# Attention on five engines: both heads of a pair in one store, and the whole order planned anew

## The chip, the cores and the metric

The kernel runs on one core of one Trainium2 chip. The metric is the device time of one execution in microseconds (us). The profile gives, for one profiled execution, every instruction's place in time on the core's engines: TensorE (PE; PEld is its weight load), VectorE (DVE), ScalarE (ACT), GpSimd (POOL), and the queue of SyncE (SP), which issues most of the DMA transfers.

## The reference

Softmax attention over 64 heads (8 x 8), each with 512 queries and keys of 64 elements:

```python
scores = np.einsum('bhqd,bhkd->bhqk', q, k) * scale
scores = scores - scores.max(axis=-1, keepdims=True)
attn = np.exp(scores)
attn = attn / attn.sum(axis=-1, keepdims=True)
return np.einsum('bhqk,bhkd->bhqd', attn, v).astype(np.float32)
```

## The kernel before

The 64 heads are worked in 32 pairs. Of each pair the kernel loads q, k and v (256 KB each, both heads, seven pairs deep), casts them to 16 bit on GpSimd, transposes q and k on TensorE (`transposes`) and copies them out of PSUM on VectorE (`copy`, tile `tqk`). A block of scores is 128 keys by 512 queries of one head. Two blocks make a *group*; there are 128 whole groups, of which the last is done in two halves. TensorE writes a group's scores to one of three PSUM buffers (`st`, line 575), and it is then exponentiated in one of two ways:

- On ScalarE, in one instruction (line 579), which writes `pt`. 112 groups go this way, three of them in the opening part (line 777).
- On VectorE, for the 16 groups listed in `Plan.ON_DVE`: `raise_` (line 599) reads the scores from PSUM and makes 16-bit integers; five passes (lines 616 to 639) make two factors, `pe` and `pd`, of them, in 16-bit data in SBUF. TensorE multiplies with both factors, so such a block costs it a second matmul.

TensorE then multiplies by v with a column of ones attached, so that each row also gets its sum (line 680). A head's result has four *units* (128 queries each); seven units share a PSUM bank, and two such banks are shared with the transposes. VectorE takes the reciprocals of the sums (line 645, `rc`) and multiplies by them (line 650), which writes into `ring`, a buffer in SBUF of `NU` = 112 units, 28 heads. From there `store` (line 658) sends heads out, in the order in which they were worked (`heads`). The last head has its own end (lines 709, 710 and 716). Heads are not always worked in the order of their numbers.

Nothing in this order is left to a scheduler. The class `Plan` steps through time with costs written into it, decides on each step what each engine does next, and returns one list of steps; the kernel then emits the steps in that order, and each engine's queue runs its instructions in just that order, waiting where data or a buffer is not there. Plan's constants hold these costs and some preferences: how late a reciprocal or a copy may be before it goes ahead of a pass (`LATE_NORM`, `LATE_COPY`), when scores are issued early (`HURRY`, `SOON`, `BACKLOG`), what a load and a store take (`LOAD`, `STORE`), and by when a cast of k and q or of v is due (`DUEK`, `DUEV`, `DUEL`). `step_sp` decides what SP issues: a load whose buffer has become free goes first, unless more than `URGENT` stores are waiting, and stores fill the places between. `room` keeps a product of line 650 from being planned before the store that frees its place in the ring. Casts on GpSimd are tied to an instruction of VectorE by `cast_behind`, since the two can hinder each other.

Of the kernel before, what the change touches and what calls it, by code (L numbers as in the profile page):

```python
# [17 lines left out]
class Plan:  # L18
# [15 lines left out]
    STEP = 5  # L34
    CALM, KEEN = 9000, 4
    FIRST_UNIT = 4
    ON_DVE = (5, 11, 15, 24, 36, 41, 49, 55, 60, 70, 76, 83, 94, 105, 109, 120)

    LATE_NORM, LATE_COPY, HURRY, SOON, BACKLOG = 2300, 700, 1000, 200, 700
    LATE_MUL, WAIT = 400, 200  # L40
    SLACK, AHEAD = 0, 2

    CAST, CAST_PORT, CAST_DONE, TO_POOL = 557, 475, 130, 150
    SCALE_PORT, PRODUCT_PORT, GAP, REACH = 271, 537, 20, 5
    FIRST_LAND, LOAD, STORE, LATENCY, ISSUE = 5200, 740, 370, 2300, 470
    QUEUED, URGENT = 3500, 16
    PAIRED = (3, 13)
    RAW, QK16, NV, NU = 7, 5, 12, 112
    PAIR, DUEK, DUEV, DUEL, PRE = 3300, 2800, 4000, 7000, 0

    def __init__(self, groups, pairs, first):
        self.groups, self.pairs = groups, pairs
        self.pe, self.act, self.dve = 7000, self.FIRST_EXP, 6300
        self.pool, self.port, self.dma = 4600, 4600, self.FIRST_LAND
        self.m, self.tiled = first, True
        self.read = []
        self.exps = {}
        for m in range(first):
            self.act += self.EXP + self.EXP_FIXED
            self.exps[m] = self.act + self.EXP_DONE  # L60
            self.read.append(self.exps[m])
        self.tq = {0: 5800}
        self.transposed = {0: 5800}
        self.next_t = 1
        self.part_t = 0
        self.banks = [5100, 5800]
        self.todo = [(g, h) for g in range(pairs) for h in range(2)]
        self.last = self.todo.pop()
        self.last_part = 0
        self.head = None  # L70
        self.units = self.FIRST_UNIT
        self.member = {b: m for m, grp in enumerate(groups) for b in grp}
        self.ready = []
        self.passes = []
        self.passed = {}
        self.raised = set()
        self.steps = []
        self.busy_dve = 0
        self.done_heads = 0

        late = {grp[0][0] for m, grp in enumerate(groups) if m in self.ON_DVE}
        due = []
        for g in range(pairs):
            scores = 5000 + self.PAIR * g
            if g:
                due += [(scores - self.DUEK, g, "k"), (scores - self.DUEK + 10, g, "q")]
            due.append((scores + self.DUEV + (self.DUEL if g in late else 0), g, "v"))
        self.due = sorted(due)
        self.uncast = list(self.due)
        self.casts = []  # L90
        self.landed, self.cast_done = {}, {}
        self.first_loads = [(g, n) for _, g, n in self.due if g < self.RAW]
        self.first_loads += [(self.RAW, "k"), (self.RAW, "q")]
        for x in self.first_loads:
            self.dma += self.LOAD
            self.landed[x] = self.dma
        self.loads, self.stores, self.stored = [], [], []
        self.sp = 1650 + 470 * len(self.first_loads)
# [55 lines left out]
    def step_sp(self, t):  # L154
        if self.sp > t or (self.loads and self.dma > t + self.QUEUED):
            return
        urgent = len(self.stores) > self.URGENT
        if self.loads and not urgent:
            g, n = self.loads[0]
            if self.cast_done.get((g - self.RAW, n), 1e9) <= t:  # L160
                self.loads.pop(0)
                self.note(t, "load", g, n)
                self.dma = max(self.dma, t + self.LATENCY - self.LOAD) + self.LOAD
                self.landed[(g, n)] = self.dma
                self.sp = t + self.ISSUE
                return
        if self.stores and self.stores[0] <= t:
            self.stores.pop(0)
            self.note(t, "store")
            self.dma = max(self.dma, t + self.LATENCY - self.STORE) + self.STORE  # L170
            self.stored.append(self.dma)
            self.sp = t + self.ISSUE

    def room(self, t, u):
        heads = (u - self.NU - self.FIRST_UNIT + 3) // 4
# [9 lines left out]
    def for_dve(self, m):  # L185
        return m in self.ON_DVE

# [69 lines left out]
    def head_values(self, t):  # L257
        if self.m <= self.KEEN:
            return False
        if self.head is None:  # L260
            for g, h in self.todo[:14]:
                if t >= self.wants(g, h, 0):
                    break
            else:
                return False
            if self.edge() and self.bank(t) is None:
                return False
            self.todo.remove((g, h))
            self.head = (g, h, 0)
        g, h, part = self.head  # L270
        if t < self.wants(g, h, part):
            return False
        if self.edge():
            n = self.bank(t)
            if n is None:
                return False
            self.banks[n] = 1e9
            self.bank_v = n
            self.begun = self.units
        self.note(t, "values", g, h, part, self.units, self.bank_v)  # L280
        more = sum(self.for_dve(self.member[(g, c, h)]) for c in range(4))
        self.full(t, self.V_UNIT + self.EXTRA * more)
        self.units += 1
        if self.edge():
            what = (self.begun, self.units - self.begun, self.bank_v)
            self.ready.append((self.pe + self.TO_DVE, "rec", what))
        self.head = (g, h, part + 1) if part < 3 else None
        return True
# [119 lines left out]
def kernel(  # L408
# [7 lines left out]
    nc = tc.nc  # L416
    B, H, S, D = q.shape
    P = 128
    NI = S // P
# [30 lines left out]
    NU = Plan.NU  # L450
    ring = cpool.tile([P, NU, D], FP32, name="ring")
# [10 lines left out]
    heads = []  # L462
# [4 lines left out]
    def source(src, g):  # L467
        b, h = g // ppb, 2 * (g % ppb)
        return src[b, h : h + 2].rearrange("h (p i) d -> p h i d", i=NI)
# [185 lines left out]
            )  # L655
        )

    def store():

        g, h, u0 = heads.pop(0)  # L660
        left = 2 * NP - 1 - (u0 + NI - Plan.FIRST_UNIT) // NI
        queue = nc.scalar if left < 2 else nc.sync
        u = u0 % NU
        if g in Plan.PAIRED and h == 0:
            return
        if g in Plan.PAIRED:
            both = ring[:, u - NI : u + NI, :].rearrange("p (h i) d -> p h i d", h=2)
            queue.dma_start(out=source(out, g), in_=both)
        else:
            queue.dma_start(out=source(out, g)[:, h], in_=ring[:, u : u + NI, :])  # L670

    def values(g, h, y, u, bank):

# [143 lines left out]
    with tc.manual_schedule():  # L817
        plan = Plan(groups, NP, 3)
        steps = plan.run()
        first_loads()  # L820
        for g, name in plan.first_loads:
            load(g, name)
        make_identity(nc, ident)
        for n in range(NV):
            nc.vector.memset(vps[n][:, :, :, D : D + 1], 1.0)
        first_pair()
        do = {
            "transposes": transposes,
            "scores": scores,
            "values": values,  # L830
            "load": load,
            "store": store,
            "cast": cast_behind,
            "raise": raise_,
            "copy": lambda g, b: copy(g),
            "pass": pass_,
            "last": last_values,
            "finish": finish,
            "rec": lambda u, n, b: reciprocal(u, n),
            "mul": lambda u, n, b: normalise(u, n),  # L840
        }
        for what, *args in steps:
            do[what](*args)
# [30 lines left out]
```

## Time and profile before

| | |
|---|---|
| three runs | 113.86, 114.5 and 114.7 us; median 114.5 |
| the profiled execution | 114.31 us, its span 112.5 us (first to last instruction) |
| granted TensorE clock | 0.999 of full speed |
| busy, PE / DVE / ACT / POOL | 104.0 / 101.3 / 105.6 / 65.2 us |
| moved | 33.84 MB, 301 GB/s over the span |

Instructions of an engine are drawn with some overlap (the next begins before the last has ended), so a group's mean duration is longer than what it holds the engine for. The latter is read from the distance between ends or from the chain of waits, which splits the time without overlap. In the slices, a 9 is a slice with 90% or more. In the timeline a row gives the start, the time to the end of the last of its instructions, the engine, the line, what it writes and reads, and how many there are; in brackets stands the idle time ahead of it and what ended that.

### The profile page before, as it was taken

To read this page: it belongs to the slowest core of one execution; us is meant where nothing else is said; L and a number is where in the kernel's file an instruction comes from. 1 tells how busy PE (TensorE), PEld (TensorE's weight loads), DVE (VectorE), ACT (ScalarE), POOL (GpSimd) and SP (SyncE) were. 2 spreads that over 40 slices of the span, in tenths; PEclk is the share of its full clock that TensorE was granted. 3 is DMA by queue.
4 is the path that set the end of the run, shared out by engine and by line. 5 is a ranking of instruction groups with operands and counts; after the bars stand their busy time and mean duration, and the time that the engine had idled before them with its cause. 6 is when DMAs were issued, how large, how long until landed. Compare 5 with 4: busy or idle time off the path is not lost.

```text
span 112.5 us, 4427 instructions
## 1 busy us (share of the span) xinstructions
PE 104.0 (92%) x1731; PEld 71.1 (63%) x1731; DVE 101.3 (90%) x226; ACT 105.6 (94%) x118; POOL 65.2 (58%) x127
## 2 busy tenths in 40 slices
PE   7988889899999998999999999999999999999970
PEld 7654546576775564657677557678667765776560
DVE  1547999999989999999999999999999999999760
ACT  4689999999999999999999999999999999999960
POOL 2166788265478866686847888755868796000000
PEclk9999999999999999999999999999999999999999
DMA  2999999999999999999999999999997976848435
GB/s 90 271 340 354 346 349 349 342 349 348 348 329 331 344 350 347 344 353 325 283 299 376 346 312 363 358 374 353 357 305 229 289 244 212 270 143 268 159 99 184
DMA packets 35349, 33.84 MB, mean 301 GB/s; under 512 B 2560, under 2 KB 35328, under 8 KB 35328
## 3 DMA queue, kind: packets, MB, share of 16 engines
q1 hardware_dynamic: 34752, 33.04, 90.8%
q10 hardware_dynamic: 576, 0.52, 1.4%
q8 instruction: 13, 0.21, 0.8%
q14 instruction: 8, 0.07, 0.2%
HBM read 25.17 MB, written 8.39 MB: 298 GB/s over the span
## 4 chain that ended last, share of the span: by engine, by line
DVE 45%; PE 42%; ACT 7%; issue 2%; DMA 1%
PE o L680 18%; PE st L575 14%; DVE pd L599 10%; DVE tqk L548 8%; DVE ring L650 8%; ACT pt L579 7%; PE tp L535 6%; DVE m L633 4%; DVE pd L639 3%; PE st_0a L727 3%; DVE pe L625 3%; DVE m L616 2%; DVE m L635 2%; DVE rc L645 2%; DMA out_dram<-ring 1%
## 5 line engine op out<-in xcount | busy, mean ns | idle before, releaser
L579 ACT ACTIVATE pt<-st 128x1024 f16<-128x1024 f32 (+1 forms) x110 | 100.3, 1114 | 0.0
L680 PEld LDWEIGHTS <-pt 128*128 128x128 f16 x880 | 38.9, 98 | 12.3 <-issue 10.6
L680 PE MATMUL o<-vp,pt 128*128 128x65 f16 x880 | 46.3, 194 | 0.2
L575 PE MATMUL st<-tqk 64*128 64x512 f16 (+1 forms) x250 | 42.4, 381 | 2.9 <-ACT pt L579 1.7
L504 POOL CAST qkp<-k 128x512 f16<-128x512 f32 x31 | 21.5, 692 | 12.2 <-DMA k<-in_k_dram 5.2
L494 POOL CAST vp<-v 128x512 f16<-128x512 f32 x32 | 21.8, 695 | 7.7 <-DVE rc L645 2.6
L504 POOL CAST qkp<-q 128x512 f16<-128x512 f32 x30 | 21.1, 703 | 6.6 <-DVE rc L645 2.2
L650 DVE TENSOR_TENSOR ring<-o,rc 128x448 f32<-128x448 f32 (+2 forms) x37 | 22.3, 606 | 0.6
L680 PE MATMUL o<-vp,pe 128*128 128x65 f16 x128 | 22.1, 195 | 0.0
L680 PE MATMUL o<-vp,pd 128*128 128x65 f16 x128 | 21.9, 193 | 0.0
L548 DVE COPY tqk<-tp 128x1024 f16<-128x1024 f16 x30 | 20.3, 677 | 0.2 <-PE tp L535 0.2
L535 PE MATMUL tp<-ident,qkp 128*128 128x128 f16 x248 | 19.5, 219 | 0.9 <-DVE ring L650 0.7
L599 DVE TENSOR_SCALAR pd<-st 128x1024 uint16<-128x1024 f32 x16 | 19.5, 1217 | 0.7 <-PE st L575 0.7
L575 PEld LDWEIGHTS <-tqk 64*128 64x128 f16 x250 | 11.7, 93 | 12.3 <-issue 4.8
L535 PEld LDWEIGHTS <-qkp 128*128 128x128 f16 x248 | 14.3, 97 | 7.3 <-issue 4.4
L680 PEld LDWEIGHTS <-pe 128*128 128x128 f16 x128 | 12.5, 97 | 3.8 <-issue 2.9
L680 PEld LDWEIGHTS <-pd 128*128 128x128 f16 x128 | 12.5, 98 | 0.0
L639 DVE TENSOR_TENSOR pd<-pd,m 128x1024 f16<-128x1024 f16 x16 | 10.9, 682 | 0.0
L633 DVE TENSOR_TENSOR m<-m 128x1024 f16<-128x1024 f16 x16 | 10.9, 681 | 0.0
L645 DVE RECIPROCAL rc<-o 128x7 f32<-128x7 f32 (+2 forms) x37 | 7.2, 195 | 1.9 <-PE o L680 1.9
L625 DVE TENSOR_SCALAR pe<-pd 128x1024 uint16<-128x1024 uint16 x16 | 6.8, 425 | 0.0
L635 DVE TENSOR_SCALAR m<-m 128x1024 f16<-128x1024 f16 x16 | 6.5, 409 | 0.0
(50 smaller groups left out, 36.6 us busy)
## 6 DMA issues: line engine op xcount, KB each, us to landing
v<-in_v_dram SPq DMA_DIRECT2D x32, 256.0 KB, 5.8
k<-in_k_dram SPq DMA_DIRECT2D x31, 256.0 KB, 5.9
q<-in_q_dram SPq DMA_DIRECT2D x31, 256.0 KB, 5.9
out_dram<-ring SPq DMA_DIRECT2D x57, 128.0 KB, 3.7
out_dram<-ring SPq DMA_DIRECT2D x2, 256.0 KB, 3.3
k<-in_k_dram ACTq DMA_DIRECT2D x2, 128.0 KB, 2.9
q<-in_q_dram SPq DMA_DIRECT2D x2, 128.0 KB, 2.7
out_dram<-ring ACTq DMA_DIRECT2D x2, 128.0 KB, 2.0
```

The costliest lines, as they stand in the source:

```text
L494: return nc.gpsimd.tensor_copy(out=vps[g % NV][:, :, :, 0:D], in_=raw[g]["v"][:, :, :, :])
L504: return nc.gpsimd.tensor_copy(out=dst, in_=src[:, :, :, :])
L535: reads[g] = nc.tensor.transpose(tps[g][:, n, i, :], qkp[g][:, n, i, :], ident)
L548: nc.vector.tensor_copy(out=tqk[g][:, :, :], in_=tps.pop(g).rearrange("p n i c -> p n (i c)"))
L575: nc.tensor.matmul(st[:, x, cols], kc, qc[:, cols], start=True, stop=True)
L579: nc.scalar.activation(out=pt[:, :, cols], in_=st[:, :, cols], func=EXP, scale=scale, bias=SHIFT)
L599: nc.vector.tensor_scalar(out=r["pd"][:, :, :], in0=r["st"][:, :, :], scalar1=BITS, scalar2=BIAS, op0=AluOp.mult, op1=AluOp.add,)
L625: ins = nc.vector.tensor_scalar(out=r["pe"][:, :, :], in0=u[:, :, :], scalar1=0x7C00, scalar2=None, op0=AluOp.bitwise_and,)
L633: ins = nc.vector.tensor_tensor(out=m16, in0=m16, in1=m16, op=AluOp.mult)
L639: ins = nc.vector.tensor_tensor(out=u16, in0=u16, in1=m16, op=AluOp.mult)
L650: nc.vector.tensor_tensor(out=ring[:, u % NU : u % NU + n, :], in0=o[:, x : x + n, 0:D], in1=rcs.pop(u)[:, 0:n].broadcast_to([P, n, D]), o ...
L680: nc.tensor.matmul(os[u // 7][:, u % 7, :], part[:, y * P : (y + 1) * P], vps[g % NV][:, h, c, :], start=(n == 0), stop=(n == len(parts) - 1),
```

## The change

In the old kernel, `store` sends each head by itself, except for two pairs fixed by number in `PAIRED`, whose first head waits for the second. In the new one Plan decides on each store whether it takes both heads of a pair: the first head must be head 0, the next one in the order of work must be head 1 of the same pair, the two must not wrap around the ring's end, and at most 18 pairs are taken so. The store is then issued once the second head is ready too, as one transfer of 256 KB. What SP needs for a store has a cost of its own (`STORE_ISSUE`).

With that the whole order was planned anew, with other constants, and with the 16 groups of VectorE at other places. All engines' orders differ; the instructions are the same in kind and number, other than the stores. The lines of the new kernel stand up to 20 further down.

```diff
-    ON_DVE = (5, 11, 15, 24, 36, 41, 49, 55, 60, 70, 76, 83, 94, 105, 109, 120)
+    ON_DVE = (5, 10, 16, 25, 28, 39, 44, 54, 63, 66, 74, 81, 91, 96, 103, 116)
-    LATE_NORM, LATE_COPY, HURRY, SOON, BACKLOG = 2300, 700, 1000, 200, 700
+    LATE_NORM, LATE_COPY, HURRY, SOON, BACKLOG = 700, 1500, 800, 160, 600
-    FIRST_LAND, LOAD, STORE, LATENCY, ISSUE = 5200, 740, 370, 2300, 470
+    FIRST_LAND, LOAD, STORE, LATENCY, ISSUE = 5200, 752, 376, 2300, 470
-    PAIRED = (3, 13)
+    PAIRED, STORE_ISSUE = 18, 520
-    PAIR, DUEK, DUEV, DUEL, PRE = 3300, 2800, 4000, 7000, 0
+    PAIR, DUEK, DUEV, DUEL, PRE = 3300, 3550, 6000, 5000, 0
...
         if self.stores and self.stores[0] <= t:
-            self.stores.pop(0)
-            self.note(t, "store")
-            self.dma = max(self.dma, t + self.LATENCY - self.STORE) + self.STORE
-            self.stored.append(self.dma)
-            self.sp = t + self.ISSUE
+            both = self.both()
+            if both and (len(self.stores) < 2 or self.stores[1] > t):
+                return
+            heads = 2 if both else 1
+            self.note(t, "store", heads)
+            self.dma = max(self.dma, t + self.LATENCY - heads * self.STORE) + heads * self.STORE
+            for _ in range(heads):
+                self.stores.pop(0)
+                self.stored.append(self.dma)
+            self.paired += heads - 1
+            self.sp = t + self.STORE_ISSUE
+
+    def both(self):
+
+        n = len(self.stored)
+        g, h, u = self.order[n]
+        return (
+            self.paired < self.PAIRED
+            and g < self.pairs - 2
+            and h == 0
+            and n + 1 < len(self.order)
+            and self.order[n + 1][0] == g
+            and u % self.NU + 8 <= self.NU
+        )
...
-    def store():
-
+    def store(both):
         g, h, u0 = heads.pop(0)
+        u = u0 % NU
+        if both == 2:
+            heads.pop(0)
+            rows = ring[:, u : u + 2 * NI, :].rearrange("p (h i) d -> p h i d", h=2)
+            nc.sync.dma_start(out=source(out, g), in_=rows)
+            return
         left = 2 * NP - 1 - (u0 + NI - Plan.FIRST_UNIT) // NI
         queue = nc.scalar if left < 2 else nc.sync
-        u = u0 % NU
-        if g in Plan.PAIRED and h == 0:
-            return
-        if g in Plan.PAIRED:
-            both = ring[:, u - NI : u + NI, :].rearrange("p (h i) d -> p h i d", h=2)
-            queue.dma_start(out=source(out, g), in_=both)
-        else:
-            queue.dma_start(out=source(out, g)[:, h], in_=ring[:, u : u + NI, :])
+        queue.dma_start(out=source(out, g)[:, h], in_=ring[:, u : u + NI, :])
```

More of the change, by code (lines that the diff above doesn't have):

```diff
@@ L78, in __init__ @@
         self.busy_dve = 0
-        self.done_heads = 0
+        self.order, self.paired = [], 0
         late = {grp[0][0] for m, grp in enumerate(groups) if m in self.ON_DVE}
@@ L269, in head_values @@
             self.head = (g, h, 0)
+            self.order.append((g, h, self.units))
         g, h, part = self.head
```

## The prediction

> **What bounds the kernel now.** I read the page first: the busy shares and the 40 slices.
>
> ```profile
> span 112.5 us, 4427 instructions
> PE 104.0 (92%) x1731; PEld 71.1 (63%) x1731; DVE 101.3 (90%) x226; ACT 105.6 (94%) x118; POOL 65.2 (58%) x127
> DVE  1547999999989999999999999999999999999760
> ACT  4689999999999999999999999999999999999960
> ```
>
> Three engines are full from the third or fourth slice to the last but two, so the shares do not yet say which one sets the end. The timeline of ScalarE does. The first two rows are from the whole run; the third is the same group of exponentials cut off at 33.1 us.
>
> ```profile
> 7.43 1.02 ACT L777 ACTIVATE pt<-st 128x1024 f16<-128x1024 f32 x1 [0.28 <-PE st L770]
> 8.35 100.29 ACT L579 ACTIVATE pt<-st 128x1024 f16<-128x1024 f32 x110
> 8.35 25.77 ACT L579 ACTIVATE pt<-st 128x1024 f16<-128x1024 f32 x28
> ```
>
> The exponential ahead of them ends at 7.43 + 1.02 = 8.45. The first 28 of line 579 end at 8.35 + 25.77 = 34.12, so one takes (34.12 - 8.45) / 28 = 0.917 us, end to end. The last ends at 108.64. From 34.12 to there stand 80 whole ones and two halves: 80 x 0.917 + 0.917 = 74.28 of the 74.52 us. ScalarE therefore loses at most 0.24 us in the whole run. It is the bound: 112 of the 128 groups go through it in both kernels, at 0.917 us each.
>
> What follows the last exponential is the last head, through lines 710 and 716:
>
> ```profile
> 109.48 0.42 DVE L710 TENSOR_TENSOR obl<-o_last,rc_last 128x256 f32<-128x256 f32 x1
> 109.93 0.33 SPq L716 DMA_DIRECT2D out_dram<-obl  x1
> ```
>
> From 108.64 to the span's end, 112.5, are 3.86 us that the diff does not touch. The start up to 8.35 is the same code too. So the new time is the old one plus what ScalarE loses newly, less at most 0.24. The sum is made against the profiled execution: 114.31 us, span 112.5 and 1.81 around it. The median of the three runs shown is 114.5 (113.86 to 114.7), 0.19 above it.
>
> **Part one: the stores.** Before, 57 transfers of 128 KB and 2 of 256 KB leave the ring on SP. The new order has 18 of 256 KB and 25 of 128 KB there, 16 fewer, and again two on ScalarE's queue. Bytes are the same.
>
> ```profile
> out_dram<-ring SPq DMA_DIRECT2D x57, 128.0 KB, 3.7
> out_dram<-ring SPq DMA_DIRECT2D x2, 256.0 KB, 3.3
> 60.06 1.02 SPq L670 DMA_DIRECT2D out_dram<-ring  x2
> 61.49 0.38 SPq L668 DMA_DIRECT2D out_dram<-ring  x1
> ```
>
> Two single issues took 1.02 us of SP, a double one 0.38: 16 x (1.02 - 0.38), some 10 us less of SP's time. Does anyone wait for it? The head written first and the one with the least room:
>
> ```profile
> 18.41 0.61 DVE L650 TENSOR_TENSOR ring<-o,rc 128x448 f32<-128x448 f32 x1
> 46.30 1.42 SPq L670 DMA_DIRECT2D out_dram<-ring  x2
> 80.95 2.78 SPq L670 DMA_DIRECT2D out_dram<-ring  x4
> 91.08 0.62 DVE L650 TENSOR_TENSOR ring<-o,rc 128x448 f32<-128x448 f32 x1
> ```
>
> Pair 0's heads are complete at 19.02 and are stored at 46.30, 27 us later. A double store adds a wait for the second head, with loads queued behind it on SP. Two heads are eight units of the ring, so at most two products of line 650 apart, and with 37 products in 112.5 us that is some 6 us, far less than those 27: the wait has ended long before its issue. At the other end, the slot of the first store in the row at 80.95 is written again at 91.08, 10.1 us later, of which 3.7 are its landing. Cover of 6 us is left. If it were gone, VectorE would stop at line 650. I cost this part at nothing, between 0 and -0.1. In the new order the first store stands behind the load of k for pair 20, before it stood behind k for pair 21, so it starts no later. The loads lie beside work as before.
>
> The Trainium skill, DMA: Bandwidth & Descriptors, Rules for kernel authors, says to coalesce small transfers, since a fixed cost of about 2 us is paid for each one. By that page 16 transfers fewer would be worth up to 32 us to whoever waited for them. Here the 256 KB landed in 3.3 us against 3.7, and nobody waits, so the sum by the page's rule is also 0.
>
> **Part two: the new order of VectorE.** This is where time can go. A group of `ON_DVE` is read out of PSUM by `raise_` (line 599). Its buffer, one of three, is needed again for the scores three groups on, and ScalarE runs dry if that is late. The work of both kernels on VectorE is the same in number (16 raises, 80 passes, 31 copies, 37 reciprocals and 37 products), but twelve of the 16 groups stand earlier than before, by up to nine groups (three stand later): the 12th is 81 where it was 83, the 15th 103 where it was 109. Raises come sooner, and VectorE has less in hand when it meets them. The chain of waits gives what each instruction holds VectorE for:
>
> ```profile
> 52.85 1.14 DVE pd L599
> ...
> 55.18 0.34 DVE m L616
> 55.52 0.33 DVE pe L625
> 55.85 0.60 DVE tqk L548
> 56.45 0.60 DVE m L633
> ...
> 57.39 0.12 DVE rc L645
> 57.50 0.29 DVE m L635
> 57.79 0.53 DVE ring L650
> 58.33 0.12 DVE rc L645
> 58.45 0.02 issue
> 58.47 0.62 DVE ring L650
> ```
>
> Raise 1.14, copy 0.60, cheap passes 0.34 and 0.33, product passes 0.60, reciprocal 0.12, ring product 0.53. Where the product follows its reciprocal at once, the pair runs from 58.33 to 59.09, 0.76 in place of 0.65: such a neighbour costs 0.11. There are 18 of these before and 13 in the new order.
>
> Now the tightest places. Before, group 109's raise:
>
> ```profile
> 92.55 1.22 DVE L599 TENSOR_SCALAR pd<-st 128x1024 uint16<-128x1024 f32 x1
> 93.63 0.62 PE L535 MATMUL tp<-ident,qkp 128*128 128x128 f16 x8
> 94.19 0.61 PE L575 MATMUL st<-tqk 64*128 64x512 f16 x4
> ```
>
> Ahead of it ScalarE has 92 exponentials of line 579, due to end at 8.45 + 92 x 0.917 = 92.81. The raise starts 0.26 ahead of that, ends at 93.77, and group 112's scores start at 94.19 behind transposes. They could start some 0.32 earlier. They take 0.39 (the row's 0.61 holds two groups), and ScalarE follows 0.1 later: 94.68, where 94 exponentials end at 94.65. So the place just fits, and the scores' 0.32 is its spare: a raise may start about 0.02 to 0.06 behind its due time before ScalarE stops. I take 0.02.
>
> The new order has ahead of raise 103, against raise 109 of before: 2 copies, 3 reciprocals, 3 products, one pass of line 616 and one of line 625 fewer, and 7 close neighbours where there were 13. That is 1.20 + 0.36 + 1.59 + 0.34 + 0.33 + 6 x 0.11 = 4.48 us less, so VectorE comes to it at 92.55 - 4.48 = 88.07. ScalarE has 86 ahead: 8.45 + 86 x 0.917 = 87.31. The raise starts 0.76 late and ScalarE loses 0.74. The other places are easier: raise 83 of before started at 71.21, and ScalarE's 69 end at 71.72; ahead of the new raise 81 stand one reciprocal, one product and six neighbours fewer and one pass more, 0.97 us less, against two exponentials fewer, 1.83. It stands 0.51 - 0.86 = -0.35: 0.35 late.
>
> ```profile
> 71.21 1.22 DVE L599 TENSOR_SCALAR pd<-st 128x1024 uint16<-128x1024 f32 x1
> 33.16 0.20 DVE L645 RECIPROCAL rc<-o 128x7 f32<-128x7 f32 x1 [0.39 <-PE o L680]
> 88.11 0.69 DVE L548 COPY tqk<-tp 128x1024 f16<-128x1024 f16 x1 [0.19 <-PE tp L535]
> ```
>
> But the 92.55 holds time in which VectorE ran out of work: 0.39 ahead of 33.16 and 0.19 ahead of 88.11, together 0.58. An engine that is later meets its inputs ready. If all of it comes back, the loss at 103 is 0.74 - 0.58 = 0.16; if none does, 0.74. ScalarE's 0.24 of before is inside 114.31 and is replaced by this loss, not added to: the change lies between 0.16 - 0.24 = -0.08 and 0.74 - 0.24 = +0.50. I take +0.2, the middle. **TensorE** has 147 switches between scores and full-width work in place of 153, six fewer; it waits for the others, so this is 0. **The casts** on GpSimd are the same 94 in another order; I cost them at nothing as well, covered by raw buffers seven pairs deep, and price the loss of that cover below.
>
> Sum: 114.31 + 0.2 = 114.5, equal to the median shown.
>
> **The rivals.** *It is hidden anyway (114.2).* The order is as good as the old one; stores never counted. For it: 10 us of room in the ring and the 0.58 that can come back. Then 114.31 - 0.08 = 114.2. Against it: ScalarE cannot give more than 0.24, so a gain of over 1%, 1.1 us, has no row behind it.
>
> *TensorE and VectorE hold each other up (116.2, slower).* Place: the two PSUM banks that carry transposes and heads, released by copies and products of VectorE. Price:
>
> ```profile
> PEld L680 <- DVE ring L650: 1.4, 6, 0.2
> DVE rc L645 <- PE o L680: 1.9, 3, 0.9
> ```
>
> TensorE already waits six times, 1.4 us in all, for a product to release a bank. With VectorE up to 1.0 us later against ScalarE (0.26 ahead, 0.76 late), each release is later too; TensorE's queue is in order, so the scores behind it wait, and the raise behind those. If these waits only double and no longer end ahead of the scores, 1.4 is added to the 0.50: 114.31 + 1.9 = 116.2. It decides from the point where VectorE's own waits between 10 and 100 us pass about 1.2 us (0.58 before). For it: in the new order the last pass of a group, as of 74 and 116, stands closer ahead of the head that reads it. Against it: TensorE idles now and has fewer switches.
>
> *VectorE meets the casts (116.0, slower).* All 94 casts hang on VectorE instructions by `cast_behind`, and all are placed anew. The rows are one of the timeline, one of the chain and two of the groups by line.
>
> ```profile
> 11.46 0.72 POOL L504 CAST qkp<-q 128x512 f16<-128x512 f32 x1
> ...
> 11.98 0.48 DVE pe L625
> ...
> L625 DVE TENSOR_SCALAR pe<-pd 128x1024 uint16<-128x1024 uint16 x16 | 6.8, 425 | 0.0
> L635 DVE TENSOR_SCALAR m<-m 128x1024 f16<-128x1024 f16 x16 | 6.5, 409 | 0.0
> ```
>
> The pass at 11.98 held VectorE 0.48 where another held it 0.33, while the cast that began at 11.46 ran beside it: 0.15. It is rare before: line 625's mean is 16 ns over line 635's, 0.26 us in 16. If ten of the 48 cheap passes met one, 1.5 us: 114.31 + 0.2 + 1.5 = 116.0. The Trainium skill, SBUF — State Buffer, Who interferes with whom, says that VectorE and GpSimd share a port pair that goes to whichever comes first for the whole instruction, while the other blocks. By that page a pass could lose a whole cast, not 0.15. The trace agrees that they collide, and shows the smaller price.
>
> **How the numbers follow.** The forecast, 114.5, has 0.53; hidden anyway 0.22; the hold-up 0.14; the casts 0.08; 0.03 is left for a gain that I cannot name. 1% of the median is 1.1 us, about what a measurement of this kernel can tell from no change. Forecast and hidden lie within it: same 0.75; the two others slower: 0.22; faster 0.03. The range starts at 113.9, the 114.2 of the hidden case less the 0.3 by which single runs of before differ from one another (113.86 to 114.7 around 114.5), and reaches to 116.0, so that it takes in the casts and about half of the hold-up. The likeliest case's own range is 114.1 to 115.0.
>
> **What would show it.** Right, if line 579 is again 110 exponentials that start near 8.35, with under 0.7 us lost to gaps, the first of them behind raises 28 to 103; if 18 issues of 256 KB stand in the table of transfers and no line 650 waits for one; if VectorE's idle time ahead of reciprocals shrinks, and the close neighbours cost less. The step with the losses is wrong, if ScalarE stops for over 1 us behind one raise, or if the waits of VectorE between 10 and 100 us grow. The forecast as a whole is wrong, if the last exponential ends before 108.3 or after 109.8, or if the time behind it is not 3.9 us.

## The result, and the profile after

| | before | after |
|---|---|---|
| median of 22 runs | 114.19 us (113.83 to 115.94) | 114.63 us (113.89 to 115.32) |
| ratio | | 1.0037, 95% interval 1.0020 to 1.0053 |
| the profiled execution | 114.31 us, span 112.5 | 114.56 us, span 112.8 |

The change makes the kernel slower by 0.37%, some 0.4 us. That lies inside the 1% that counted as no difference in the prediction, and its number was near (114.5), yet two steps that led to it were wrong. From the page and the transfer table of the kernel after:

```profile
span 112.8 us, 4401 instructions
PE 102.6 (91%) x1731; PEld 69.0 (61%) x1731; DVE 101.2 (90%) x226; ACT 105.8 (94%) x118; POOL 66.2 (59%) x127
DVE  1558999999999999999999999999999999996470
ACT  4799999999999999999999999999999999999940
out_dram<-ring SPq DMA_DIRECT2D x18, 256.0 KB, 5.6
out_dram<-ring SPq DMA_DIRECT2D x25, 128.0 KB, 2.5
out_dram<-obl SPq DMA_DIRECT2D x1, 128.0 KB, 2.5
q14 instruction: 8, 0.07, 0.2%
```

Nothing in the shares tells of a loss: no engine but GpSimd, which has time to spare, is busy for more than 0.2 us longer. The third of the transfer rows does. The store of the last head, `obl`, takes 2.5 us from issue to landing. Before, the same store took 1.8 (the second row is the last reciprocal of before):

```profile
out_dram<-obl SPq DMA_DIRECT2D x1, 128.0 KB, 1.8
109.27 0.17 DVE L709 RECIPROCAL rc_last<-o_last 128x4 f32<-128x4 f32 x1
```

ScalarE's line and the end, from the timeline of the kernel after:

```profile
7.55 10.27 ACT L599 ACTIVATE pt<-st 128x1024 f16<-128x1024 f32 x11
98.95 9.46 ACT L599 ACTIVATE pt<-st 128x1024 f16<-128x1024 f32 x11
108.81 0.18 DVE L727 RECIPROCAL rc_last<-o_last 128x4 f32<-128x4 f32 x1
109.02 0.42 DVE L728 TENSOR_TENSOR obl<-o_last,rc_last 128x256 f32<-128x256 f32 x1
109.47 0.33 SPq L734 DMA_DIRECT2D out_dram<-obl  x1
```

The last exponential ends at 98.95 + 9.46 = 108.41, 0.23 earlier than before. The last reciprocal then starts 0.40 behind it, where it was 0.63 (109.27 - 108.64): before, VectorE began the product of the head ahead of it only at 108.93, now at 108.34. The store is issued 1.06 behind the last exponential, where it was 1.29 (109.93 - 108.64). So at the issue the new kernel is 0.46 us ahead. Then it loses 0.65 until the last packet of the store has arrived (2.07 behind the issue, 1.42 before) and 0.06 in the closing steps: -0.23 - 0.23 + 0.65 + 0.06 = +0.25, the difference of the two profiled executions. The loss stands wholly behind the last instruction that computes anything.

The packets show what happens there. While the last store is written, the queue called q14, which the page lists as one for instructions, fetches a block of 8 KB. In the kernel after, that fetch starts 0.90 us behind the store's issue and takes 0.82. Of the store's 16 completion writes, all but one have arrived 1.36 behind the issue; the last comes at 2.07. Before, the block was fetched 1.54 us ahead of the issue, and the 16 writes arrived together, by 1.42.

### The profile page after: what moved, and what is told of

Its sections match the earlier page's. It is cut to its first block, busy times and chain, and to the rows that moved or that the text cites. A ratio compares the mean times of both kernels' runs of the same rounds, so it can differ in the third digit from the quotient of the medians.

```text
span 112.8 us, 4401 instructions
## 1 busy us (share of the span) xinstructions
PE 102.6 (91%) x1731; PEld 69.0 (61%) x1731; DVE 101.2 (90%) x226; ACT 105.8 (94%) x118; POOL 66.2 (59%) x127
## 4 chain that ended last, share of the span: by engine, by line
DVE 33%; PE 27%; DMA 18%; issue 8%; POOL 7%; ACT 4%; POOLq 0%
PE o L698 11%; DMA out_dram<-ring 9%; DMA q<-in_q_dram 9%; PE st L595 8%; DVE pd L619 7%; DVE tqk L568 6%; DVE ring L670 5%; POOL qkp L524 4%; ACT pt L599 4%; DVE pd L659 3%; PE tp L555 3%; DVE m L653 3%; POOL vp L514 3%; PE st_0a L745 3%; DVE pe L645 2%
## 5 line engine op out<-in xcount | busy, mean ns | idle before, releaser
L698 PE MATMUL o<-vp,pt 128*128 128x65 f16 x880 | 45.3, 194 | 0.7 <-POOL vp L514 0.4
L595 PE MATMUL st<-tqk 64*128 64x512 f16 (+1 forms) x250 | 41.4, 380 | 2.6 <-ACT pt L599 1.1
L524 POOL CAST qkp<-k 128x512 f16<-128x512 f32 x31 | 22.6, 730 | 12.2 <-DMA k<-in_k_dram 5.0
L514 POOL CAST vp<-v 128x512 f16<-128x512 f32 x32 | 21.3, 677 | 9.1 <-PE st L595 3.6
L524 POOL CAST qkp<-q 128x512 f16<-128x512 f32 x30 | 21.7, 722 | 7.8 <-DVE rc L665 5.3
L595 PEld LDWEIGHTS <-tqk 64*128 64x128 f16 x250 | 10.4, 93 | 11.3 <-issue 4.0
```

Of the source, the lines that this page charges most:

```text
L514: return nc.gpsimd.tensor_copy(out=vps[g % NV][:, :, :, 0:D], in_=raw[g]["v"][:, :, :, :])
L524: return nc.gpsimd.tensor_copy(out=dst, in_=src[:, :, :, :])
L595: nc.tensor.matmul(st[:, x, cols], kc, qc[:, cols], start=True, stop=True)
L698: nc.tensor.matmul(os[u // 7][:, u % 7, :], part[:, y * P : (y + 1) * P], vps[g % NV][:, h, c, :], start=(n == 0), stop=(n == len(parts) - 1),
```

## The experiments

Two theories for the loss at first: *the order* (VectorE meets its groups later, so that ScalarE's line ends later) and *the stores* (256 KB transfers, or their places). The third came out of the traces: *the fetch*, an instruction block that meets the last store. Each ratio is to the kernel before on the same chip, with its 95% interval.

### Both kernels again, and each half of the change by itself

*The kernel before, and the kernel after, unchanged.*

> The kernel of before, profiled once more. Theory 'order': ScalarE's line of 110 exponentials has under 0.3 us of gaps whenever it starts at 7.5 or at 8.35, and the end stays 3.9 us behind the last one; time 114.2. Theory 'opening': the start of the line moves by up to 0.8 us from run to run with TensorE's clock, and an earlier start gives gaps in this order too, 0.3 to 0.8 us before 45 us. Theory 'end': the last transfer's landing varies, so 3.9 to 4.4.

> The changed kernel, profiled once more. Theory 'order': again 0.5 to 0.9 us of gaps in ScalarE's line, all before 45 us; time 114.6, 0.3 to 0.5 us over before. Theory 'opening': if its line starts at 8.35, the gaps fall under 0.3 us. Theory 'end': the end again 4.4 us behind the last exponential, and this, not the gaps, is the difference to before.

*The old order, with 18 pairs merged.* The order of everything is kept. Where the two stores of a pair stand next to each other on SP, the first is left out and the second takes both heads.

```diff
-        if g in Plan.PAIRED and h == 0:
+        if g in merged and h == 0:
...
+            if h == 0 and g1 == g and near and u % NU + 2 * NI <= NU and len(merged) < 18:
+                merged.add(g)
```

> The kernel of before with its order kept, but 18 pairs leave the ring in one transfer, where two single stores of one pair stand together on SP. Theory 'order': as before, 114.2, within 0.15 us. Rival 'stores': 0.3 to 0.5 us slower, 114.6.

*The new order, with each double store as two single ones at the same place.*

```diff
-            rows = ring[:, u : u + 2 * NI, :].rearrange("p (h i) d -> p h i d", h=2)
-            nc.sync.dma_start(out=source(out, g), in_=rows)
+            for x in range(2):
+                rows = ring[:, u + NI * x : u + NI * x + NI, :]
+                nc.sync.dma_start(out=source(out, g)[:, x], in_=rows)
```

> The changed kernel with its order kept to the instruction, but each of the 18 double stores issued as two single ones at the same place (16 issues more on SP). Theory 'order': as the changed kernel, 114.6, within 0.15 us. Rival 'stores': the 256 KB transfers hold up loads or the end, and the time goes back to 114.2.

| | ratio | last exponential ends, us | from there to the end, us |
|---|---|---|---|
| before again | 0.9997 (0.9973 to 1.0020) | 108.62 | 3.89 |
| old order, 18 merged | 1.0005 (0.9979 to 1.0031) | 108.34 | 3.89 |
| after again | 1.0026 (0.9998 to 1.0055) | 108.24 | 4.14 |
| new order, all single | 1.0060 (1.0035 to 1.0085) | 108.35 | 4.53 |

Merged stores alone change nothing that can be measured, as the prediction had it. The loss comes with the new order, and yet ScalarE's line ends no later in it; what is longer is the time behind it. In the new order the single stores came out 0.34% slower still, which neither expectation had (the order: no change; the stores: a gain). The two intervals overlap; the pair with four copies below gives 0.45% the same way. Part of that can be read:

```profile
out_dram<-ring SPq DMA_DIRECT2D x61, 128.0 KB, 4.2
109.41 0.33 SPq L735 DMA_DIRECT2D out_dram<-obl  x1
SPq L888 <- DMA out_dram<-obl: 2.0, 1, 2.0
```

These rows are of the new order with single stores: transfers, timeline, waits. At its end SP waits for each group of transfers in turn. With the other number of transfers the last store reports through a semaphore that stands early in that list, so that four more waits of some 0.06 us come behind it: from the last packet to the end it took 1.50 us, in the kernel after 1.24. The other 0.15 us or so was not traced to a place.

### Moving the fetch

The instructions of the two kernels are not quite the same in number: ScalarE's program has 69 separate wait instructions in the new order, where it had 73, a by-product of which waits could be folded into other instructions. If the block belongs to ScalarE and is fetched when the engine reaches a certain instruction, four instructions fewer let it come some four instructions later. So: the kernel after with four and with eight tiny copies (128 x 1) on ScalarE in the opening, the same with single stores and four copies, and the kernel before with three instructions fewer there.

```diff
+        small = cpool.tile([P, 16], FP32, name="small")
+        def pad(n0, n1):
+            for n in range(n0, n1):
+                nc.scalar.copy(small[:, n : n + 1], ones[:, n : n + 1])
...
+        pad(0, 4)
         nc.scalar.copy(q16[:, 0, 2:4], twice(0, 2, 2))
...
         nc.scalar.copy(k16[:, 1], tk[:, 1])
+        pad(4, 8)
```

This is the edit with eight; with four the two calls are `pad(0, 2)` and `pad(2, 4)`.

> The changed kernel with four tiny copies more in ScalarE's queue during its opening waits, so that this queue has 200 instructions like before, in place of 196. Theory 'fetch': the 8 KB instruction fetch that starts at 110.2 to 110.4 us in the changed order belongs to ScalarE's queue and comes a fixed number of its instructions in; it moves 2 us ahead, to about 108.2, the last store lands 1.4 us behind its issue in place of 1.9 to 2.1, the end stands 3.65 us behind the last exponential, and the time is 114.0. Rival 'stores': the late landing comes from the stores or the order, so it stays at 4.1 to 4.4 and the time at 114.5.

> The same with eight tiny copies. Theory 'fetch': the fetch moves 4 us ahead, to about 106.3; the end as with four, 3.65 us; time 114.0 to 114.1. Rival 'stores': 4.1 to 4.4 us, 114.5. If the copies themselves cost time in the opening, this one shows it twice over.

> The changed order with single stores (as in the kernel that split them) and with the four tiny copies. Theory 'fetch': the end at 3.65 to 4.0 us behind the last exponential in place of 4.5. What the double stores are worth in this order is the difference to the kernel with four copies alone: 0 if splitting did nothing but share the late fetch, 0.4 to 0.5 us if single stores cost by themselves (the split one stood at 1.006 of before, the changed one at 1.003).

The kernel before with three fewer: two opening casts go to GpSimd and one load of k to SP.

```diff
+        nc.scalar.dma_start(out=tk[:, 0], in_=source(k, 0)[:, 0])
         for h in range(2):
-            nc.scalar.dma_start(out=tk[:, h], in_=source(k, 0)[:, h])
             nc.sync.dma_start(out=tq[:, h], in_=source(q, 0)[:, h])
+        nc.sync.dma_start(out=tk[:, 1], in_=source(k, 0)[:, 1])
...
-        nc.scalar.copy(q16[:, 1, 0:2], twice(1, 0, 2))
-        nc.scalar.copy(k16[:, 1], tk[:, 1])
+        nc.gpsimd.tensor_copy(out=q16[:, 1, 0:2], in_=twice(1, 0, 2))
+        nc.gpsimd.tensor_copy(out=k16[:, 1], in_=tk[:, 1])
```

> The kernel of before with three instructions fewer in ScalarE's queue: two of its opening casts on GpSimd, one of its two loads on SP (the opening itself may shift by 0.1 to 0.4 us). Theory 'fetch': the fetch moves from 108.4 to about 110.0 and the last store lands 1.9 to 2.1 us behind its issue in place of 1.41; the end 4.3 to 4.5 us behind the last exponential in place of 3.89; time 114.6 to 114.8. Rival 'stores': the landing stays at 1.41 and the end at 3.89.

The table has the packets of the profiled executions up to here, in us from the issue of the last store: when the fetch starts, how long it takes, when 15 of the 16 completion writes are in, and the last one.

| kernel | fetch starts | takes | 15 writes | last | last exponential to end | ratio |
|---|---|---|---|---|---|---|
| before | -1.54 | 0.72 | 1.39 | 1.42 | 3.89 | 1 |
| before again | -1.56 | 0.71 | 1.39 | 1.41 | 3.89 | 0.9997 |
| old order, merged | -1.56 | 0.74 | 1.39 | 1.41 | 3.89 | 1.0005 |
| before, 3 fewer | **0.96** | 0.60 | 1.41 | **1.90** | 4.49 | 1.0049 (1.0022 to 1.0077) |
| after | **0.90** | 0.82 | 1.36 | **2.07** | 4.37 | 1.0037 |
| after again | **0.89** | 0.66 | 1.37 | **1.90** | 4.14 | 1.0026 |
| after, all single | **0.98** | 0.64 | 1.36 | **1.97** | 4.53 | 1.0060 |
| after, 4 copies | -0.97 | 0.78 | 1.37 | 1.75 | 4.01 | 0.9990 (0.9959 to 1.0021) |
| all single, 4 copies | -0.95 | 0.64 | 1.35 | 1.62 | 4.10 | 1.0035 (1.0006 to 1.0065) |
| after, 8 copies | -2.92 | 0.63 | 1.35 | 1.37 | 3.62 | 0.9966 (0.9938 to 0.9993) |

In every row 15 of the 16 shares are in at 1.35 to 1.41. The last is late when the fetch comes during the store or up to 1 us ahead of it, and not late when it comes 1.5 us ahead or more.

The packets also show how. A share of the last store is eight packets of 1 KB. In the four rows in bold the fetch is over at 1.56, 1.72, 1.55 and 1.63, and the last eight packets of the store start at 1.55, 1.72, 1.55 and 1.62 and follow one another, while all others are in: they wait for the fetch. The trace does not name a packet's engine; that the eight wait on the one that fetches is read from these times. In the two rows with four copies the fetch is over 0.18 and 0.31 ahead of the store's issue, and the delay is handed on. The last store on ScalarE's queue has its last eight packets in at 1.40 and 1.27, where without a fetch near it all were in by 0.8, and the last eight of `obl` start just then. So with four copies the end came at 4.01, not at the 3.65 that was expected.

It works both ways. The old order, with three instructions fewer on ScalarE, gets the late share (1.90) and becomes slower by 0.5%; its opening is another too, but the last exponential ended only 0.17 later and the time behind it is 0.60 longer. The new order, with eight instructions more, loses the late share, and with it the whole of the change's loss.

### Is it the place of the fetch, or the copies?

> The changed kernel with eight tiny ScalarE copies in the opening, once more, to see whether its lead over the kernel before (0.9966) holds. Theory of the instruction fetch: the last 8 KB fetch comes near 107 us, ahead of the last store, the time behind the last exponential is 3.6 to 3.7 us, ratio to the kernel before 0.997 (113.9). Rival, that the lead was chance: ratio 0.999 to 1.002.

> The changed kernel with twelve tiny copies (208 instructions on ScalarE). Theory of the fetch: once the last fetch is ahead of the last store, going further brings nothing more; fetch near 103 us, time behind the last exponential 3.6 us, ratio 0.997. Rival, that the extra copies themselves bring time (a later start of ScalarE, a warmer TensorE): another 0.2 to 0.3% less than with eight, ratio 0.994. Rival, that each copy costs its own time on the bound: ratio 0.999 to 1.000.

The kernel before with the same eight copies:

> The kernel before with the same eight copies: the control. Theory of the fetch: its last fetch was harmless at 108.4 us and now comes at some 100 us, so the time behind the last exponential stays at 3.9 us and the ratio is 1.000 (114.2). Rival, that the copies bring time by themselves: ratio 0.996, as in the changed kernel.

> The changed kernel unchanged, beside the padded ones on the same chip. Theory of the fetch: last fetch at 110.2 to 110.4 us, time behind the last exponential 4.1 to 4.4 us, ratio 1.003, that is 0.5% over the one with eight copies. Rival, that padding does nothing: the same ratio as the one with eight copies, within 0.2%.

| | fetch starts | last write | last exponential to end | ratio |
|---|---|---|---|---|
| after, 8 copies | -2.92 | 1.37 | 3.61 | 0.9983 (0.9937 to 1.0028) |
| after, 12 copies | -4.69 | 1.36 | 3.60 | 0.9983 (0.9946 to 1.0021) |
| before, 8 copies | -5.86 | 1.42 | 3.89 | 1.0000 (0.9961 to 1.0039) |
| after | 0.89 | 1.88 | 4.10 | 1.0007 (0.9973 to 1.0041) |

The times behind the last exponential are as the fetch theory has them: no more gain from twelve than from eight, none in the kernel before. The fetch moved less far than expected, to 105.7 us with twelve copies (103 expected) and to 104.7 in the kernel before (100 expected). The intervals of these ratios are too wide to decide, and the 0.5% expected between the last row and the first came out as 0.24%. A stall in the opening, which some executions of either order have, adds to the spread. Here are the timeline rows of the kernel before with eight copies, where 1.04 us is lost ahead of 9.78: the cast of k had waited for its load, and the scores behind it came late:

```profile
7.25 0.61 POOL L504 CAST qkp<-k 128x512 f16<-128x512 f32 x1 [3.38 <-DMA k<-in_k_dram]
7.70 1.04 ACT L579 ACTIVATE pt<-st 128x1024 f16<-128x1024 f32 x1
9.78 99.45 ACT L579 ACTIVATE pt<-st 128x1024 f16<-128x1024 f32 x109 [1.04 <-PE st L575]
```

So the two controls and the pair itself were run on one chip: eight copies at the end of ScalarE's program, and eight in the opening but on GpSimd.

```diff
         nc.sync.dma_start(out=source(out, LAST)[:, 1], in_=ob[:, :, :])
+        small = cpool.tile([P, 16], FP32, name="small")
+        for n in range(8):
+            nc.scalar.copy(small[:, n : n + 1], ones[:, n : n + 1])
```

> The changed kernel with the same eight tiny ScalarE copies, but behind everything else that ScalarE does. The number of instructions is that of the version with the copies in the opening (204), the position of every other instruction is that of the changed kernel. Theory that the position of an instruction in ScalarE's program sets when the last 8 KB fetch comes: fetch again at 110.2 to 110.4 us, or the fetch is gone only if it belonged to the end of the program; time behind the last exponential 4.1 to 4.4 us, ratio to the kernel before 1.001 to 1.004, some 0.5% over the version with the copies in the opening. Rival, that the number of instructions alone counts: fetch near 107 us, 3.6 us, ratio 0.997.

```diff
-                nc.scalar.copy(small[:, n : n + 1], ones[:, n : n + 1])
+                nc.gpsimd.tensor_copy(out=small[:, n : n + 1], in_=ones[:, n : n + 1])
```

> The changed kernel with eight tiny copies in the opening on GpSimd in place of ScalarE. Theory of the fetch by ScalarE's position: nothing moves there, fetch at 110.2 to 110.4 us, 4.1 to 4.4 us behind the last exponential, ratio 1.001 to 1.004. Rival, that any disturbance of the opening brings the gain of the eight copies: ratio 0.997.

> The changed kernel with eight tiny ScalarE copies in the opening, beside its two controls and the changed kernel itself. Theory of the fetch: 3.6 us behind the last exponential; the ratio lies 0.4 to 0.6% under those of the three others. Rival, that the fetch costs nothing: within 0.2% of the others.

> The changed kernel unchanged, for the direct ratio to the padded one on one chip. Theory of the fetch: 4.1 to 4.4 us behind the last exponential, ratio to the kernel before 1.001 to 1.004, 0.4 to 0.6% over the padded one. Rival: equal to the padded one within 0.2%.

| | fetch starts | takes | last write | last exponential to end | ratio |
|---|---|---|---|---|---|
| after | 0.91 | 0.68 | 1.94 | 4.28 | 1.0039 (1.0006 to 1.0071) |
| 8 copies on GpSimd | 0.90 | 0.83 | 2.07 | 4.32 | 1.0031 (1.0004 to 1.0058) |
| 8 copies at ScalarE's end | 0.52 | 0.31 | 1.67 | 3.93 | 0.9984 (0.9961 to 1.0007) |
| 8 copies in the opening | -2.92 | 0.73 | 1.37 | 3.60 | 0.9965 (0.9937 to 0.9992) |

Copies on another engine change nothing, so it is ScalarE's program. Copies at its end leave the fetch at 110.14 us, during the store, and the copies in the opening move it to 106.56: the position decides, and the number alone does not. But the copies at the end were also cheaper than the position theory had said. Their fetch began 0.4 earlier and took 0.31 where the others took 0.6 to 0.8, so it delayed the last share by 0.3 only, and the ratio went down with it. Why that block came quicker stays open.

The first profiled execution of the kernel after and the last row of this table make the plainest pair, since they issue the last store at 109.47 and 109.48. The window rows are the kernel after, then the one with eight copies in the opening; the last two columns are the share of 16 DMA engines and GB/s. Below the second pair stand that kernel's span and the issue and landing of its last store.

```profile
109.80:110.80 1.00, 0.00 (x0) 0.00 (x0) 0.00 (x0) 0.00 (x0) 0.00 (x0) 1.00 0.79 253
110.90:111.50 0.60, 0.00 (x0) 0.00 (x0) 0.00 (x0) 0.00 (x0) 0.00 (x0) 1.00 0.04 14
```

```profile
109.80:110.80 1.00, 0.00 (x0) 0.00 (x0) 0.00 (x0) 0.00 (x0) 0.00 (x0) 1.00 0.78 255
110.90:111.50 0.60, 0.00 (x0) 0.00 (x0) 0.00 (x0) 0.00 (x0) 0.00 (x0) 0.98 0.00 0
span 112.0 us, 4409 instructions
109.48 0.33 SPq L734 DMA_DIRECT2D out_dram<-obl  x1
out_dram<-obl SPq DMA_DIRECT2D x1, 128.0 KB, 1.7
```

Up to 110.8 both move the same. From 110.9 the one is done; in the other a share of 0.04 is still busy, which is 0.6 of one engine in 16, and the end of the program waits for it.

**Without the late share.** The kernel after with eight copies in the opening was measured three times: 0.9966 (0.9938 to 0.9993), 0.9983 (0.9937 to 1.0028) and 0.9965 (0.9937 to 0.9992) of the kernel before, 113.85, 114.34 and 113.94 us. Two of the three intervals exclude 1. So without the late share the new order is perhaps 0.2 to 0.35% faster than the old one, and the fetch cost more than that. In the profiled executions this gain does not stand in ScalarE's line, which ended at 108.66, 108.78 and 108.42, about where the kernel before ended it, but behind it: 3.60 to 3.62 us in place of 3.89.

## Why the prediction came out as it did

**"From 108.64 to the span's end ... are 3.86 us that the diff does not touch": wrong, and this is the step that failed.** The code behind the last exponential is the same, its time is not: 4.37, 4.14, 4.10 and 4.28 in the four profiled executions of the kernel after. Two terms are in it. VectorE reaches the last head 0.23 us sooner after the last exponential, and the store lands 0.46 to 0.65 later. The prediction took unchanged code for unchanged time, and so put the late share at nothing. It had named this as its own test: the time behind the last exponential was to be 3.9 us.

**The fetch had a row that the prediction did not read.** The transfer table of before has the instruction queues too. How much they move is nothing (0.2%); what counts is when. The Trainium skill, Runtime: NRT & Kernel Launch, section Instruction fetch mechanics, says that the sequencer fetches the next page of instructions through a DMA queue of its own while it executes the current one, and calls the cost mostly hidden. The trace agrees on the queue, and no loss was traced to the fetches up to 91 us. It differs at the end, where one cost 0.46 to 0.65 us, and in the size: that page has 16 KB, the blocks that moved with ScalarE's program here were of 8 KB.

**VectorE at raise 103, +0.2 in the sum: wrong in its sign.** The prediction had the raise 0.76 late and took the middle of -0.08 to +0.50. Measured, from VectorE's and ScalarE's timelines of the kernel after:

```profile
86.95 1.22 DVE L619 TENSOR_SCALAR pd<-st 128x1024 uint16<-128x1024 f32 x1
17.99 69.28 ACT L599 ACTIVATE pt<-st 128x1024 f16<-128x1024 f32 x75 [0.17 <-PE st L595]
```

The 11 exponentials quoted above and these 75 make 86, and they end at 17.99 + 69.28 = 87.27; the raise starts 0.32 ahead of that. In the three other executions of the kernel after it is 0.32 to 0.33 ahead. That is 1.08 us better than worked out. The sum is plainest in the fourth execution, which began its opening nearly as the kernel before did: from the first raise to this one VectorE took 77.53 us where it had taken 83.11, so 5.58 less and not 4.48. All of the 0.58 us in which VectorE had waited came back (the prediction's own favourable end). The other 0.5 is work between the raises that the sum undercounted: measured from start to start, the three products of the ring fewer gave 2.26 us, not 1.59 (0.39 of it such a wait), and the pass of line 645 fewer 0.64, not 0.33. So the line ended at 108.24 to 108.41 in four executions, where the kernel before ended it at 108.62 and 108.64: 0.2 to 0.4 earlier, beyond the bracket's lower end of -0.08. How much of that is the order's is not shown, since the old order with merged stores ended its line at 108.34 too, after a first raise at 9.12 in place of 9.43.

**Where gaps come.** The prediction expected the first behind raises 28 to 103, under 0.7 us in all. The profiled execution of the kernel after lost 0.77, at 17.99, 24.6, 27.5, 29.3 and 41.3, and nothing at raises 74 to 103. The largest wait rows of TensorE beside the usual ones:

```profile
PE st L595 <- DVE pd L619: 0.6, 1, 0.6
PE o L698 <- POOL vp L514: 0.4, 1, 0.4
```

One is raise 28, as expected, but ScalarE lost only 0.03 by it, at 29.3. The other, a cast of v that came late, was not expected, and the largest gap, 0.27 at 17.99, follows it. These gaps cost the end little. This execution started its line at 7.55, 0.80 earlier than before, and gave that lead back; another of the same kernel started at 8.20, had no gap at all, and ended at 108.28, 0.13 earlier.

**The stores: right, for the old order.** With 18 pairs merged in it the ratio is 1.0005. No line 670 waits for a store, and 18 transfers of 256 KB stand in the table. In the new order the prediction's zero is off by 0.34 to 0.45% in favour of merging (1.0060 against 1.0026, 1.0035 against 0.9990), of which the closing waits explain 0.22 to 0.26 us of about 0.4. The Trainium skill, DMA: Bandwidth & Descriptors, Rules for kernel authors, from which the prediction drew up to 32 us, calls transfers under 64 KB mostly overhead. Those here are of 128 KB, so that estimate was more than the rule says.

**The rivals.** *Hidden anyway* was right that ScalarE's line loses nothing, and took the end of the run for unchanged like the forecast. *TensorE and VectorE hold each other up* did not happen, though VectorE's waits between 10 and 100 us were its test:

```profile
103.95 0.21 DVE L665 RECIPROCAL rc<-o 128x7 f32<-128x7 f32 x1 [0.99 <-PE o L698]
PEld L698 <- DVE ring L670: 1.2, 4, 0.5
```

Between 10 and 100 us the profile shows no wait of VectorE; the first one for a head stands at 103.95, past the last raise at 97.52. TensorE's waits for products went from 1.4 us to 1.2. *VectorE meets the casts* did happen, at two places of this execution. From its chain of waits:

```profile
15.12 1.00 DVE pd L659
22.32 0.64 DVE pe L645
```

Elsewhere these passes hold VectorE for 0.60 and at most 0.33. Beside the first a cast ran from 14.97 to 15.58, beside the second one from 21.76 to 22.68, as drawn. Together they cost some 0.7 us, which is why this execution took 78.20 us from the first raise to raise 103 and the fourth, without these two, 77.53. The prediction also read its own example wrongly. The 0.15 at 11.98 was no smaller price than the rest of the cast: that cast was drawn to 12.18, so only 0.20 of it was left. With 0.36 left a pass lost 0.31 or more, with 0.46 left 0.40: what it loses is about what is left of the cast. At the end of the line this cost at most the 0.13 above, and none of the rivals held the loss behind the last exponential.

So the near number, 114.5 against 114.63, is luck, two errors of about the same size: a loss of 0.2 where ScalarE's line and the last head together won 0.46, and no loss at the end, where 0.65 and 0.06 in the closing steps stood. And "equal to the median shown" rested on a median of three runs; over 22 the kernel before stands at 114.19, so that the same sum would have meant a loss of 0.3 us. In the four comparisons the ratio was 1.0007 to 1.0039, 0.1 to 0.45 us; the +0.25 of the profiled pair lies between. What the single runs of one kernel spread over (1.4 to 2.1 us) is not explained by the fetch; the opening's stall of 1 us is a part of it, and the rest stays open.

## What to carry to other kernels

Here the time behind the last computation was set by a transfer, and so by what shared its engines at that moment: when the code of the tail is unchanged but an engine's instructions before it are not, check where the last block of instructions is fetched. When a small change loses a few tenths of a per cent, first take the difference apart at the end of the line that bounds the kernel (before it, behind it), since both sides can move with opposite signs. A reordering can be judged only after such accidents of place are taken out, here by a few instructions that do nothing.

## What was not expected of the hardware

- The last 8 KB fetch of ScalarE's instructions took 0.31 to 0.83 us and held up one of the 16 shares of a 128 KB store beside it or just behind it: the last share came at 1.62 to 2.07 us where the other 15 were in at 1.35 to 1.41.
- The fetch follows the position in ScalarE's program. Four tiny copies in the opening, some 100 us earlier, moved it from 0.9 us behind the last store's issue to 0.97 ahead of it, eight to 2.92 ahead.
- The start of ScalarE's line differs between executions of one kernel (7.55 to 8.49 in the kernel after and its variants), and its end does not follow: the execution that began at 7.55 ended at 108.41, one that began at 8.20 at 108.28.
- SP's closing waits run one by one, some 0.06 us each, and where the last transfer's semaphore stands among them was worth 0.22 to 0.26 us.
- A VectorE pass that started while a GpSimd cast ran lost about what was left of the cast: 0.15 of 0.20 us, 0.31 or more of 0.36, 0.40 of 0.46.
